# A mixture-of-experts trunk layer on one core: routing's order, low parts on GpSimd, and two weight slots opened earlier

## The chip, the core and the metric

The program runs on one core of one Trainium2 chip. The metric is the device time of one execution in microseconds, given as the median of several runs. The engines are called TensorE (PE in the rows), VectorE (DVE), ScalarE (ACT), GpSimd (POOL) and SyncE (SP, which here issues the weights' DMAs); PEld is TensorE's weight load, and a q behind a name (SPq, ACTq) is the queue of that engine, DMA issues above all.

## The reference

One layer works on 512 latent tokens of 1024 features, with 256 context tokens beside them. What lies ahead of the change is the normed input projection, three token mixers and their gated merge. The part around the change is the output projection with its residual, the second norm, the routing and the experts:

```python
mix_l = merge_branches((pool, att_l, rwo_l), gate_l, w_br[l], w_out[l])   # ... merged @ w_out
x = x + mod[:, 2] * mix_l
f_l = modulate(x, norm2_g[l], mod[:, 3], mod[:, 4]).reshape(B * L, D)     # rms_norm(x, g) * (1 + scale) + shift
x = x + mod[:, 5] * hier_moe(f_l, w_rg, w_re, w_g, w_u, w_d)

def hier_moe(h, ...):
    lg = h @ w_rg                                  # 4 groups: the best one
    grp = argmax(lg); p_grp = softmax(lg)[grp]
    le = (h @ w_re).reshape(T, 4, 8)[grp]          # 8 experts in it: the best two
    top_v, top_i = top_k(le, 2)
    gates = p_grp * softmax(top_v)
    # each chosen expert: (silu(x @ w_g[e]) * (x @ w_u[e])) @ w_d[e], times its gate, summed by token
```

There are 32 experts; each has w_g and w_u of 1024 x 512 and w_d of 512 x 1024, float32, so 6 MB a piece and 201 MB in all.

## The kernel before, in words

**The sum.** The merged branches stand transposed in SBUF, split in a high part `mgh` (in two of the weight slots, the names ew_8461 and ew_8462 in rows) and a low part `mgl` (tiles mq), each 8 blocks of 128 features by 512 tokens. The output projection is `out_mm` (L1446 before): for four column blocks of 256, `wo[0]` to `wo[3]`, and four groups of 128 tokens (t = 0 to 3) it adds three products per block k, high x high, low x high and high x low. `out_add` (L1452 to L1454) multiplies by the gate row, adds to the residual `xt2[t]` and lets ScalarE sum the squares of these 256 columns (`sq`). Blocks 2 and 3 of the weights lie in the tiles xn0 and xn1.

**Routing.** `turned` transposes the four (later the next four) 128 x 128 blocks of token group t on TensorE (L1369), and ScalarE copies them (L1370) to `fT[t]`, a tile of the ring F (5 buffers, pool `wfa`). `logits` (L1376) multiplies them by the router's weights. `route` takes rsqrt on GpSimd (L104), scales the logits (L1385) and chooses the group and two experts in a row of small VectorE operations up to L1401. `count` (L1409, L1410) gives each token its place in its expert's 64 rows. `normed` (L1436, L1437, L1440, L1441) writes the normed tokens as a high and a low part to xn0 (t = 0, 1) or xn1 (t = 2, 3), and a plain copy in an F tile to `x_d` in DRAM, from which later experts' tokens are gathered. xn1 is free only when the last column block's matmuls are done. For the first four experts, tokens are not gathered but chosen by matmuls with a one-hot matrix (`chosen` L1500, `rows_of` L1506), scaled by `put` and given to the experts.

**The experts' weights.** `load` issues one half of one matrix of one expert (128 x 2048 floats) on SP's queue (L1257). Thirteen places take turns by the list RING: slots ew0 to ew7 in one pool, ew8 and ew9 where `mgh` lies, ew10 and ew11 in a pool `peq` that is opened where `mgl` and the ring F lay, and place 12 in two tiles of another ring. Two further halves (SPARE) go into tiles that the experts need only later (oh, yhl, xT). `fetch(n)` issues up to the n-th half; after the first round each place is filled again when its expert's matmuls are done. `up` (L1608) is an expert's first product, `down` (L1643) its last.

**What sets the order.** The program is written in order and a scheduler places each instruction in its engine's queue; `tc.high_priority(n)` lets what is written inside it stand ahead of other work, the more the greater n. Each engine works its queue in order. SP's queue is in the order in which the loads are written.

Of the kernel before, what the change touches and what calls it, by code (L numbers as in the profile page):

```python
# [9 lines left out]
FT = mybir.dt.float32  # L10
# [68 lines left out]
def trunk_kernel(ctx: ExitStack, tc: tile.TileContext, I, out, dbg=None, upto=99):  # L79
# [665 lines left out]

    pb = ctx.enter_context(ExitStack())
    TW = dict(bufs=1, reuse_waits="tile")
    pf_ = ctx.enter_context(ExitStack())

    wfb = ctx.enter_context(tc.tile_pool(name="rmapg", side="right", **TW))  # L750
    wfa = pf_.enter_context(tc.tile_pool(name="rmapf", side="right", **TW))

    class Ring:
        n = 0
# [468 lines left out]
    m5 = xpool2.tile([128, D], FT)  # L1223
    m2 = mgp.tile([128, D], FT, name="m2", bufs=1)

    RING = (4, 5, 6, 7, 12, 0, 1, 2, 3, 8, 9, 10, 11)
    NS = len(RING)

    SPARE = (4, 5)
# [199 lines left out]
    def normed(t):  # L1429

        if t % 2 == 0:
            xns.append(xnp.tile([128, 2, 2, D], FR, name=f"xn{t // 2}"))
        hi, lo = xns[t // 2][:, 0, t % 2], xns[t // 2][:, 1, t % 2]
        for h in range(2):
            sl = slice(h * 512, h * 512 + 512)
            S.activation(hi[:, sl], xt2[t][:, sl], AF.Copy, scale=ss[:, t, 3:4])  # L1436
        V.scalar_tensor_tensor(lo, xt2[t], ss[:, t, 3:4], hi.bitcast(FT), op0=OP.mult, op1=OP.subtract)  # L1437

        xf = wfa.tile([128, D], FT, name="F", bufs=7 - FB)
        S.activation(xf, xt2[t], AF.Copy, scale=ss[:, t, 3:4])  # L1440
# [53 lines left out]
    def gather(b):  # L1494

        oh = (ep if b else xnp).tile([128, 4, EB, 64], FR, name="oh", bufs=1)
        ohf = oh.rearrange("p t e s -> p t (e s)")

        def chosen(t):
            return V.tensor_tensor(oh[:, t], slot[:, t, b * EB:b * EB + EB, None].to_broadcast([128, EB, 64]),  # L1500
                                   io1[:, None, :].to_broadcast([128, EB, 64]), OP.is_equal)

        def rows_of(p, k, ts):
            for t in ts:
                for a in range(2):
                    PE.matmul(p, xns[t // 2][:, a, t % 2, k * 128:k * 128 + 128], ohf[:, t], start=(t == 0 and a == 0),  # L1506
                              stop=(t == 3 and a == 1))

        def put(k, p):
            if k % 2:  # L1510
                S.activation(xT[:, k], p, AF.Identity, scale=g2c[:, k:k + 1], bias=s2c[:, k:k + 1])
            else:
                V.tensor_scalar(xT[:, k], p, g2c[:, k:k + 1], s2c[:, k:k + 1], op0=OP.mult, op1=OP.add)

        if b == 0:

            ahead = {}
            for t in range(3):
                chosen(t)
                yield  # L1520
            for k in range(AH):
                ahead[k] = ps_big()[:, 0:EB * 64]
                rows_of(ahead[k], k, range(3))
            chosen(3)
            yield
            xT = ep.tile([128, KD, EB * 64], FT, name="xT")
            for k in range(KD):
                p = ahead[k] if k in ahead else ps_big()[:, 0:EB * 64]
                rows_of(p, k, (3,) if k in ahead else range(4))
                put(k, p)  # L1530
            yield xT, *slots(b, oh)
            return
        for t in range(4):
            chosen(t)
        yield
        gc, ix = slots(b, oh)
        ii = ep.tile([128, EB // 2], U32, name="ii")
# [7 lines left out]
        xT = ep.tile([128, KD, EB * 64], FT, name="xT")  # L1545
# [12 lines left out]
    nxt = gather(0)  # L1558
    for t in range(4):
        p = ps_big()[:, 0:256]  # L1560
        for k in range(KD):
            out_mm(p, wo[2], t, k)
        turned(t, 0, 4)
        out_add(p, t, 2)
    for t in range(5):
        if t < 4:
            p = ps_big()[:, 0:256]
            for k in range(KD):
                out_mm(p, wo[3], t, k)
            out_add(p, t, 3)  # L1570
        if t:
            with tc.high_priority(0):
                turned(t - 1, 4, 4)
                logits(t - 1, 0, 8)
                if t > 1:
                    count(t - 2)
                route(t - 1)
            normed(t - 1)
        if t > 1:
            next(nxt)  # L1580
# [5 lines left out]
    if upto < 7:  # L1586
        return
    dump("slot", slot)
    fetch(11)
    gates()  # L1590
    m2x.close()
    mgx.close()
    pf_.close()
    peq = ctx.enter_context(tc.tile_pool(name="expq", side="right", **TW))
    fetch(NS)
    epx = ctx.enter_context(ExitStack())
    ep = epx.enter_context(tc.tile_pool(name="experts", bufs=2, reuse_waits="tile"))
    tgx = ep.tile([128, 4, NE // 2, 6], FR, bufs=1)

    tp = tg.rearrange("p t (q e) -> p t q e", e=2)  # L1600
# [4 lines left out]
    def up(xT, w, pg, i):  # L1605
        for k in range(KD):
            for h in range(2):
                PE.matmul(pg[64 * h:64 * h + 64, i], xT[:, k], of(w[i], k)[:, h * 256:h * 256 + 256],  # L1608
                          start=(k == 0), stop=(k == KD - 1), tile_position=(0, 64 * h))

    def hidden(pg, pool):
# [43 lines left out]
    def parts_of(y, h, rows, pool, name="yhl", eng=G):  # L1655

        sl = slice(h * 512, h * 512 + 512)
        yhl = pool.tile([rows, 2, 512], FR, name=name, bufs=1)
        yh, yl = yhl[:, 0], yhl[:, 1]
        S.activation(yh, y[:, sl], AF.Copy)  # L1660
        eng.tensor_sub(yl, y[:, sl], yh.bitcast(FT))  # L1661
        return sl, yh, yl

    def combine(y, ix, last=False):

        oT = oT_
        V.tensor_scalar(oT, iol, ix, None, op0=OP.is_equal)
        if last:
            yield
            with tc.high_priority(100):  # L1670
                pts = [parts_of(y, h, 128, ep, *(("oh", G) if h else ("yhl", V))) for h in range(2)]
# [6 lines left out]
        pt_ = parts_of(y, 0, 128, ep)  # L1678
        yield
        for t in range(4):  # L1680
            add(oT, t, *pt_)
        pt_ = parts_of(y, 1, 128, ep)
        yield
        for t in range(4):
            add(oT, t, *pt_)
# [1 line left out]
    def store(t):  # L1687
        nc.sync.dma_start(out[t * 128:(t + 1) * 128], xt2[t])

    load(SPARE[0], *(ep.tile([128, 1, D], FT, name=nm, bufs=1) for nm in ("oh", "yhl")))  # L1690
    load(SPARE[1], ep.tile([128, 2, D], FT, name="xT"))
# [15 lines left out]
    for e in range(NE + 1):  # L1707
        fetch(NS + max(0, 6 * e - 2) - (2 if e > 1 else 0))
        j = e % EB
        if e < NE:  # L1710
            if j == 0:
                got[e // EB] = cur
                nxt = gather(e // EB + 1) if e + EB < NE else iter(())
            xT = got[e // EB][0][:, :, j * 64:j * 64 + 64]
# [37 lines left out]
    with tc.If(nmost > 64):  # L1752
        for t in range(4):
            if t % 2 == 0:
                xns.append(xnp.tile([128, 2, 2, D], FR, name=f"xn{t // 2}"))
            xf = op_.tile([128, D], FT, name="xf")
            nc.sync.dma_start(xf, x_d[t * 128:(t + 1) * 128])
            S.activation(xns[-1][:, 0, t % 2], xf, AF.Copy)
            V.tensor_sub(xns[-1][:, 1, t % 2], xf, xns[-1][:, 0, t % 2].bitcast(FT))
        with tc.For_i(0, NE, 1) as e:  # L1760
# [12 lines left out]
            with tc.For_i(0, 7, 1):  # L1773
# [18 lines left out]
                y = op_.tile([64, D], FT)  # L1792
                pg = ps_big().rearrange("p (i n) -> p i n", i=2)
                up(xT, wo, pg, 0)
                up(xT, wo, pg, 1)
                down(turn_(hidden(pg, op_), op_), wo, gc, y, 0)
                oT = op_.tile([64, 512], FR)
                pt = ps_sm()[0:64]
# [1 line left out]
                    PE.transpose(pt[:, t * 128:t * 128 + 128], oh[:, t].bitcast(FT), ident)  # L1800
                S.activation(oT, pt, AF.Copy)
                for h in range(2):
                    pt_ = parts_of(y, h, 64, op_)
                    for t in range(4):
                        add(oT, t, *pt_)
        for t in range(4):
# [114 lines left out]
```

## Time and profile before

| what | value |
|---|---|
| runs | 1447.19, 1440.27 and 1447.98 us; median 1447.19 us |
| the profiled execution | 1448.53 us, span 1446.6 us |
| busy share: TensorE, its weight load, VectorE, ScalarE, GpSimd | 94%, 70%, 57%, 33%, 26% |
| moved by DMA | 399.96 MB, 276 GB/s over the span |
| mean granted TensorE clock | 0.977 of full speed |

The span is the time from the first to the last instruction on the core; the rest of an execution lies around it. A busy share is a mean over stages that have different limits: up to some 970 us the mixers and the sum run, behind that the experts.

### The profile page before, as it was taken

Reading aid. Unit: us, or ns where it says so; the run is one execution under the profiler, and the core shown is the slowest. Engines: PE = TensorE matmul, PEld = TensorE weight load, DVE = VectorE, ACT = ScalarE, POOL = GpSimd, SP = SyncE. Lnnn points to the kernel's source line nnn. Section 1 sums busy time; section 2 is a strip of 40 time slices with the busy share of each in tenths; the row PEclk is TensorE's granted clock in tenths of the full one; section 3 lists DMA queues with packets and bytes.
Section 4 is the critical chain, followed back from the end, with each engine's and each line's share of the span. In section 5 each row is a group of like instructions: output and inputs, shape, how many; then the busy total and the mean of one; then the engine's idle time right before and its main releaser. Section 6 shows DMA issues by size and latency. Waiting matters only on the chain.

```text
span 1446.6 us, 24032 instructions
## 1 busy us (share of the span) xinstructions
PE 1362.2 (94%) x9148; PEld 1018.7 (70%) x9148; DVE 822.0 (57%) x1673; ACT 482.5 (33%) x1089; POOL 382.5 (26%) x345
## 2 busy tenths in 40 slices
PE   5999999998999999799999998999999999999897
PEld 3786788887888888688887776985555554555443
DVE  4553327779988958266776886462433433333334
ACT  4432235665565632144445523341111111111101
POOL 2111155445432444112221257110101101111001
PEclk9999999999999999799999999999999999999999
DMA  9368755666566466965847276579999999999996
GB/s 367 151 216 309 236 181 171 215 210 199 193 217 217 179 206 214 252 209 159 260 136 240 85 259 234 204 277 417 419 418 418 419 419 419 419 418 419 419 419 241
DMA packets 138038, 399.96 MB, mean 276 GB/s; under 512 B 38757, under 2 KB 69477, under 8 KB 107200
## 3 DMA queue, kind: packets, MB, share of 16 engines
q1 hardware_dynamic: 101920, 331.55, 61.9%
q10 hardware_dynamic: 32400, 58.60, 11.1%
q0 software_dynamic: 3600, 8.24, 1.7%
q8 instruction: 74, 1.21, 0.3%
q14 instruction: 44, 0.36, 0.1%
HBM read 343.44 MB, written 58.72 MB: 278 GB/s over the span
## 4 chain that ended last, share of the span: by engine, by line
PE 42%; DMA 25%; DVE 8%; issue 3%; ACT 2%; POOL 1%; SPq 1%; ACTq 0%; DVEq 0%; POOLq 0%
DMA ew<-in_w_eu_dram 9%; DMA ew<-in_w_ed_dram 5%; PE pp L220 5%; PE pp L1608 5%; DMA ew<-in_w_eg_dram 4%; PE pp L1152 3%; PE pp L1446 3%; PE pp L1643 2%; PE pp L234 2%; PE sc L1007 2%; PE pp L825 1%; PE pp L812 1%; PE sc L1006 1%; DMA F<-in_w_eg_dram 1%; PE pp L818 1%
## 5 line engine op out<-in xcount | busy, mean ns | idle before, releaser
L1608 PE MATMUL pp<-ew,xT 128*64 128x256 f32 x1888 | 225.0, 383 | 14.4 <-DMA ew<-in_w_eu_dram 9.4
L1608 PEld LDWEIGHTS pp<-ew,xT 128*64 128x64 f32 x1888 | 132.0, 137 | 97.4 <-issue 18.5
L220 PE MATMUL pp<-xlh,wh 128*128 128x512 f32 x344 | 135.7, 405 | 1.3 <-ACT wide L413 1.3
L220 PE MATMUL pp<-xll,wh 128*128 128x512 f32 x344 | 135.7, 395 | 0.4 <-POOL xll L320 0.4
L220 PE MATMUL pp<-xlh,wl 128*128 128x512 f32 x344 | 135.1, 393 | 0.0
L1661 POOL TENSOR_TENSOR yhl<-m,yhl 128x512 fp32r<-128x512 f32 x30 | 38.2, 1272 | 364.0 <-ACT yhl L1660 364.0
L215 POOL TENSOR_TENSOR wl<-wraw,wh 128x512 fp32r<-128x512 f32 x84 | 113.4, 1377 | 64.1 <-ACT wh L214 59.9
L1653 DVE TENSOR_TENSOR x<-x,pp 128x512 f32<-128x512 f32 x128 | 80.7, 681 | 41.6 <-PE pp L1652 41.5
L1643 PE MATMUL pp<-ew,hT 128*64 128x512 f32 x440 | 101.0, 599 | 0.0
L1614 DVE TENSOR_TENSOR hh<-hh,pp 128x256 f32<-128x256 f32 x32 | 13.5, 421 | 148.1 <-ACT hh L1613 148.1
L1646 DVE SCALAR_TENSOR_TENSOR m<-pp,gc,m 64x512 f32<-64x512 f32 x62 | 46.5, 750 | 63.3 <-PE pp L1643 62.6
L220 PEld LDWEIGHTS pp<-xlh,wh 128*128 128x128 f32 x344 | 64.7, 190 | 20.8 <-issue 5.6
L214 ACT ACTIVATE wh<-wraw 128x512 fp32r<-128x512 f32 (+1 forms) x112 | 61.1, 612 | 54.1 <-PE pp L220 51.7
L220 PEld LDWEIGHTS pp<-xll,wh 128*128 128x128 f32 x344 | 65.2, 190 | 15.1 <-issue 2.0
L220 PEld LDWEIGHTS pp<-xlh,wl 128*128 128x128 f32 x344 | 65.2, 189 | 13.8
L1643 PEld LDWEIGHTS pp<-ew,hT 128*64 128x64 f32 x440 | 29.0, 136 | 55.9 <-issue 50.9
L234 PE MATMUL pp<-wh,xlh 128*128 128x256 f32 x192 | 59.5, 310 | 5.1 <-ACT qo L659 2.3
L806 POOL TENSOR_TENSOR ao<-ar,cst 128x512 f32<-128x512 f32 x24 | 30.8, 1284 | 124.3 <-PE pp L818 68.3
L1622 ACT ACTIVATE hT<-psm 128x256 f32<-128x256 f32 x32 | 12.3, 384 | 149.7 <-PE psm L1620 144.2
L1613 ACT ACTIVATE hh<-pp 128x256 f32<-128x256 f32 x32 | 12.3, 384 | 139.9 <-PE pp L1608 139.9
L234 PE MATMUL pp<-wl,xlh 128*128 128x256 f32 x192 | 57.7, 300 | 0.0
L234 PE MATMUL pp<-wh,xll 128*128 128x256 f32 x192 | 57.5, 299 | 0.0
(436 smaller groups left out, 3133.4 us busy)
## 6 DMA issues: line engine op xcount, KB each, us to landing
ew<-in_w_eg_dram SPq DMA_DIRECT2D x59, 1024.0 KB
ew<-in_w_eu_dram SPq DMA_DIRECT2D x58, 1024.0 KB
ew<-in_w_ed_dram SPq DMA_DIRECT2D x56, 1024.0 KB
wraw<-in_w_in_dram SPq DMA_DIRECT2D x27, 1024.0 KB
u_d<-ub ACTq DMA_DIRECT2D x16, 1152.0 KB
wada<-in_w_adr_dram SPq DMA_DIRECT2D x16, 1024.0 KB
ar<-u_d SPq DMA_DIRECT2D x24, 640.0 KB
wa<-in_w_ad_dram SPq DMA_DIRECT2D x8, 1024.0 KB
```

The costliest lines, as they stand in the source:

```text
L214: S.activation(self.h[:, kk, :n], raw[:, kk, :n], AF.Copy)
L215: (eng[q % 2] if type(eng) is tuple else eng).tensor_sub(self.l[:, kk, :n], raw[:, kk, :n], self.h[:, kk, :n].bitcast(FT))
L220: PE.matmul(ps, a[:, k, cs], b[part][:, k], start=(k + n == 0), stop=(k == KD - 1 and n == 2))
L234: PE.matmul(ps, a[part][:, k, ts], b[:, k], start=(n == 0), stop=(n == 3 * KD - 1))
L806: G.tensor_mul(ao, aa[:, :, 2:3].to_broadcast([128, 4, 2, 64]), offm[:, None].to_broadcast([128, 4, 2, 64]))
L1152: PE.matmul(ps, a[:, k], bs[k][:, x], start=(c == 0), stop=(c == 11))
L1446: PE.matmul(p, a[:, ts], x[:, k], start=(k == 0 and c == 0), stop=(k == KD - 1 and c == 2))
L1608: PE.matmul(pg[64 * h:64 * h + 64, i], xT[:, k], of(w[i], k)[:, h * 256:h * 256 + 256], start=(k == 0), stop=(k == KD - 1), tile_position= ...
L1643: PE.matmul(pd[64 * h:64 * h + 64], hT[:, k], of(w[2], k)[:, h * 512:h * 512 + 512], start=(k == 0), stop=(k == 3), tile_position=(0, 64 * h))
L1646: V.scalar_tensor_tensor(y[ps_, h * 512:h * 512 + 512], pd[64 * h:64 * h + 64], gc, m5[ps_, h * 512:h * 512 + 512], op0=OP.mult, op1=OP.mult)
L1653: V.tensor_add(xt2[t][:, sl], xt2[t][:, sl], p)
L1661: eng.tensor_sub(yl, y[:, sl], yh.bitcast(FT))
```

## The change

Four groups of edits.

1. The low parts' products with the last column block's weights (`mgl` x `wo[3][0]`, 32 matmuls) are done first, ahead of block 2, into four accumulators that stay open; the high parts follow block 2. With that `mgl` is read out after block 2, its pool is closed there and `peq` opened, and `fetch(11)` stands there and no longer behind the routing. Slots 10 and 11 come ahead of 8 and 9 in RING.
2. The priority of the routing's second half (`turned`, `logits`, `count`, `route`) rises from 0 to 100, and that of `chosen(3)` and the first experts' rows to 200.
3. The low parts of tokens 2 and 3 (`normed`) are made by GpSimd in two halves, out of the F tile and the high part, and no longer by VectorE.
4. The ring F stays open to the end; the experts' transposed tokens (`xT`, now two tiles for each of two turns), the low and high parts of an expert's result (`yhl`) and one of the spare halves lie in it.

```diff
-    RING = (4, 5, 6, 7, 12, 0, 1, 2, 3, 8, 9, 10, 11)
+    RING = (4, 5, 6, 7, 12, 0, 1, 2, 3, 10, 11, 8, 9)
...
-        V.scalar_tensor_tensor(lo, xt2[t], ss[:, t, 3:4], hi.bitcast(FT), op0=OP.mult, op1=OP.subtract)
+        if t < 2:
+            V.scalar_tensor_tensor(lo, xt2[t], ss[:, t, 3:4], hi.bitcast(FT), op0=OP.mult, op1=OP.subtract)
...
         S.activation(xf, xt2[t], AF.Copy, scale=ss[:, t, 3:4])
+        if t > 1:
+            for h in range(2):
+                sl = slice(h * 512, h * 512 + 512)
+                G.tensor_sub(lo[:, sl], xf[:, sl], hi[:, sl].bitcast(FT))
         nc.scalar.dma_start(x_d[t * 128:(t + 1) * 128], xf)
...
-            chosen(3)
+            with tc.high_priority(200):
+                chosen(3)
             yield
-            xT = ep.tile([128, KD, EB * 64], FT, name="xT")
-            for k in range(KD):
-                p = ahead[k] if k in ahead else ps_big()[:, 0:EB * 64]
-                rows_of(p, k, (3,) if k in ahead else range(4))
-                put(k, p)
+            xT = xTs[b % 2]
+            with tc.high_priority(200):
+                for k in range(KD):
+                    p = ahead[k] if k in ahead else ps_big()[:, 0:EB * 64]
+                    rows_of(p, k, (3,) if k in ahead else range(4))
+                    put(k, p)
...
     nxt = gather(0)
+
+    pss = [ps_big()[:, 0:256] for _ in range(4)]
     for t in range(4):
-        p = ps_big()[:, 0:256]
+        for k in range(KD):
+            PE.matmul(pss[t], mgl[k][:, t * 128:t * 128 + 128], wo[3][0][:, k], start=(k == 0), stop=False)
+    for t in range(4):
+        p = (ps_sm() if t else ps_big())[:, 0:256]
         for k in range(KD):
             out_mm(p, wo[2], t, k)
         turned(t, 0, 4)
         out_add(p, t, 2)
+    mgx.close()
+    peq = ctx.enter_context(tc.tile_pool(name="expq", side="right", **TW))
+    fetch(11)
     for t in range(5):
         if t < 4:
-            p = ps_big()[:, 0:256]
             for k in range(KD):
-                out_mm(p, wo[3], t, k)
-            out_add(p, t, 3)
+                for c in range(2):
+                    PE.matmul(pss[t], mgh[k][:, t * 128:t * 128 + 128], wo[3][c][:, k], start=False,
+                              stop=(k == KD - 1 and c == 1))
+            out_add(pss[t], t, 3)
         if t:
-            with tc.high_priority(0):
+            with tc.high_priority(100):
                 turned(t - 1, 4, 4)
                 logits(t - 1, 0, 8)
...
-    fetch(11)
     gates()
     m2x.close()
-    mgx.close()
-    pf_.close()
-    peq = ctx.enter_context(tc.tile_pool(name="expq", side="right", **TW))
     fetch(NS)
...
+    spare = wfa.tile([128, 1, D], FT, name="F", bufs=7 - FB)
+    xTs = [[wfa.tile([128, KD // 2, EB * 64], FT, name="F", bufs=7 - FB) for _ in range(2)] for _ in range(2)]
+    yhl_ = []
```

On ScalarE's queue, this is the stretch from token 1's norm to the store of token 3, before. F<-psm is a copy of transposed rows, xn_9623 the tile of tokens 2 and 3's high parts, F<-x a plain normed copy, x_d<-F its store, sq a sum of squares:

```order
L1440 ACTIVATE F<-x_8917,ss 128x1024
L1454 ACTIVATE sq,ss<-x_8918 128x256
L1441 DMA x_d<-F 128x1024
L1440 ACTIVATE F<-x_8918,ss 128x1024
L1441 DMA x_d<-F 128x1024
L1436 ACTIVATE xn_9623<-x_8918,ss 128x512 x2
L1696 DMA m_9817<-in_iota_dram 128x512
L1454 ACTIVATE sq,ss<-x_8918 128x256
L1370 ACTIVATE F<-psm 128x512 x2
L1436 ACTIVATE xn_9623<-x_8918,ss 128x512 x2
L1440 ACTIVATE F<-x_8918,ss 128x1024
L1441 DMA x_d<-F 128x1024
```

and after:

```order
L1458 ACTIVATE sq,ss<-x_8918 128x256
L1440 ACTIVATE F<-x_8917,ss 128x1024
L1445 DMA x_d<-F 128x1024
L1717 DMA m_9821<-in_iota_dram 128x512
L1458 ACTIVATE sq,ss<-x_8918 128x256
L1435 ACTIVATE xn_9631<-x_8918,ss 128x512 x2
L1440 ACTIVATE F<-x_8918,ss 128x1024
L1435 ACTIVATE xn_9631<-x_8918,ss 128x512 x2
L1440 ACTIVATE F<-x_8918,ss 128x1024
L1445 DMA x_d<-F 128x1024
L1369 ACTIVATE F<-psm 128x512 x2
L1445 DMA x_d<-F 128x1024
```

The copies of the transposed rows of tokens 2 and 3 (L1370 before, L1369 after) stood ahead of token 3's norm; they now stand behind both norms and a store.

On SP's queue, these are the weights from the place where two loads wait for the sum, up to the first load into a slot used a second time (the last row), before; ew is a slot, mosti the counts that SP reads:

```order
L1257 DMA ew_9714<-in_w_eg_dram 128x2048
L1257 DMA ew_9716<-in_w_eu_dram 128x2048
L1257 DMA ew_9738<-in_w_eu_dram 128x2048
L1257 DMA ew_9740<-in_w_ed_dram 128x2048
L1257 DMA oh<-in_w_ed_dram 128x1024
L1257 DMA yhl<-in_w_ed_dram 128x1024
L1257 DMA xT<-in_w_ed_dram 128x2048
L1751 TENSOR_LOAD mosti
L1751 ISA x2
L1257 DMA ew_9867<-in_w_ed_dram 128x2048
```

and after:

```order
L1256 DMA ew_9429<-in_w_eg_dram 128x2048
L1256 DMA ew_9431<-in_w_eu_dram 128x2048
L1256 DMA ew_9739<-in_w_eu_dram 128x2048
L1256 DMA ew_9741<-in_w_ed_dram 128x2048
L1256 DMA F<-in_w_ed_dram 128x1024 x3
L1256 DMA oh<-in_w_ed_dram 128x1024
L1772 TENSOR_LOAD mosti
L1772 ISA x2
L1256 DMA ew_9871<-in_w_ed_dram 128x2048
```

The first two rows were slots 8 and 9, free when the whole sum is done, and are now slots 10 and 11, free when the low parts are read; slots 8 and 9 follow. The spares stand behind all of these in both, and the load into a slot used again behind the counts.

On GpSimd's queue, the stretch from the norms' rsqrt to the first gather, before:

```order
L104 TENSOR_TENSOR ss<-ss,nhalf 128x1 x4
L1701 MEMSET xn_9820 128x2048
L1701 MEMSET xn_9821 128x2048
L1541 DMA xn_9821<-x_d,ii 128x1024 x2
L1661 TENSOR_TENSOR yhl<-m_9916,yhl 128x512 x2
```

and after:

```order
L104 TENSOR_TENSOR ss<-ss,nhalf 128x1 x4
L1444 TENSOR_TENSOR xn_9631<-F,xn_9631 128x512 x4
L1722 MEMSET xn_9824 128x2048
L1722 MEMSET xn_9825 128x2048
L1548 DMA xn_9825<-x_d,ii 128x1024 x2
```

Four subtractions of 128 x 512 (L1444) stand behind the four rsqrt; on VectorE's queue two operations of 128 x 1024 (L1437) are gone.

## Rows read from the trace of the kernel before

**Rows 1.** The windows, whole core: busy us, instructions, TensorE clock, DMA share, GB/s

```profile
925.00:950.00 25.00, 25.00 (x217) 25.00 (x215) 11.89 (x40) 12.26 (x27) 1.64 (x3) 1.00 0.26 104
950.00:975.00 25.00, 24.20 (x204) 21.44 (x204) 17.12 (x77) 9.60 (x17) 4.11 (x3) 1.00 0.86 331
975.00:1000.00 25.00, 24.93 (x185) 14.61 (x181) 6.32 (x18) 1.92 (x5) 2.16 (x2) 1.00 1.01 417
...
1300.00:1400.00 100.00, 92.89 (x612) 49.78 (x614) 36.05 (x62) 12.82 (x27) 10.89 (x9) 1.00 1.01 419
```

**Rows 2.** The timeline of SP, the weights' queue, 922 to 971 us

```profile
922.23 26.73 SPq L1257 DMA_DIRECT2D ew<-in_w_eg_dram  x2
950.96 10.73 SPq L1257 DMA_DIRECT2D ew<-in_w_eu_dram  x2
...
963.43 0.43 SPq L1257 DMA_DIRECT2D xT<-in_w_ed_dram  x1
970.90 0.34 SPq L1257 DMA_DIRECT2D ew<-in_w_ed_dram  x1
```

**Rows 3.** The chain of waits, 935 to 972 us: start, length, what

```profile
935.07 5.70 PE pp L1446 x48
...
953.36 0.61 ACT F L1370
954.01 1.10 PE pp L1376 x8
955.13 0.27 DVE lgs L1385
...
955.99 1.28 DVE xn L1437
...
960.79 1.08 PE psm L1409 x8
...
968.99 3.17 PE pp L1608 x27
```

**Rows 4.** The timeline of ScalarE, 938 to 976 us

```profile
940.29 1.34 ACT L1436 ACTIVATE xn<-x,ss 128x512 fp32r<-128x512 f32 x2 [0.85 <-POOL ss L104]
941.54 1.14 ACT L1440 ACTIVATE F<-x,ss 128x1024 f32<-128x1024 f32 x1
...
942.70 0.33 ACTq L1441 DMA_DIRECT2D x_d<-F  x1
943.05 0.41 ACT L1454 ACTIVATE sq<-x 128x256 f32<-128x256 f32 x1
943.36 0.19 ACT L1454 ACTIVATION_READ_ACCUMULATOR sq<-x 128x1 f32 x1
...
950.96 0.72 ACT L1436 ACTIVATE xn<-x,ss 128x512 fp32r<-128x512 f32 x1 [1.30 <-PE pp L1446]
```

**Rows 5.** The timeline of VectorE, 936 to 970 us

```profile
937.95 0.42 DVE L1452 TENSOR_TENSOR tm<-pp,m 128x256 f32<-128x256 f32 x1 [1.42 <-PE pp L1446]
...
957.19 0.25 DVE L1385 SCALAR_TENSOR_TENSOR lgs<-pp,ss,lb 128x36 f32<-128x36 f32 x1
```

**Rows 6.** The timeline of VectorE, one operation at two places

```profile
223.69 0.14 DVE L666 TENSOR_SCALAR st<-st 128x4 f32<-128x4 f32 x1
...
331.43 1.23 DVE L666 TENSOR_SCALAR st<-st 128x4 f32<-128x4 f32 x1
```

**Rows 7.** The timeline of GpSimd at the second of these places

```profile
329.87 2.77 POOL L215 TENSOR_TENSOR wl<-wraw,wh 128x512 fp32r<-128x512 f32 x2
```

**Rows 8.** The page's costliest groups, GpSimd's subtraction of the experts

```profile
L1661 POOL TENSOR_TENSOR yhl<-m,yhl 128x512 fp32r<-128x512 f32 x30 | 38.2, 1272 | 364.0 <-ACT yhl L1660 364.0
```

**Rows 9.** The windows around an idle TensorE, columns as in rows 1

```profile
880.40:883.60 3.20, 0.00 (x0) 0.00 (x0) 3.13 (x5) 1.15 (x2) 3.20 (x3) 0.86 0.57 182
883.60:886.10 2.50, 2.06 (x4) 1.25 (x5) 0.47 (x1) 0.63 (x1) 2.50 (x2) 0.50 0.37 108
...
889.50:893.00 3.50, 3.50 (x16) 2.89 (x16) 3.01 (x4) 1.50 (x3) 1.45 (x2) 1.00 0.29 75
```

More of the change, by code (lines that the diff above doesn't have):

```diff
@@ L747, in trunk_kernel @@
     TW = dict(bufs=1, reuse_waits="tile")
-    pf_ = ctx.enter_context(ExitStack())
     wfb = ctx.enter_context(tc.tile_pool(name="rmapg", side="right", **TW))
-    wfa = pf_.enter_context(tc.tile_pool(name="rmapf", side="right", **TW))
+    wfa = ctx.enter_context(tc.tile_pool(name="rmapf", side="right", **TW))
     class Ring:
@@ L1509, in put @@
         def put(k, p):
+            x = xT[k // 4][:, k % 4]
             if k % 2:
-                S.activation(xT[:, k], p, AF.Identity, scale=g2c[:, k:k + 1], bias=s2c[:, k:k + 1])
+                S.activation(x, p, AF.Identity, scale=g2c[:, k:k + 1], bias=s2c[:, k:k + 1])
             else:
-                V.tensor_scalar(xT[:, k], p, g2c[:, k:k + 1], s2c[:, k:k + 1], op0=OP.mult, op1=OP.add)
+                V.tensor_scalar(x, p, g2c[:, k:k + 1], s2c[:, k:k + 1], op0=OP.mult, op1=OP.add)
         if b == 0:
@@ L1544, in gather @@
         yield
-        xT = ep.tile([128, KD, EB * 64], FT, name="xT")
+        xT = xTs[b % 2]
         for k in range(0, KD, 2):
@@ L1607, in up @@
             for h in range(2):
-                PE.matmul(pg[64 * h:64 * h + 64, i], xT[:, k], of(w[i], k)[:, h * 256:h * 256 + 256],
+                PE.matmul(pg[64 * h:64 * h + 64, i], xT[k], of(w[i], k)[:, h * 256:h * 256 + 256],
                           start=(k == 0), stop=(k == KD - 1), tile_position=(0, 64 * h))
@@ L1653, in add, with parts_of @@
         V.tensor_add(xt2[t][:, sl], xt2[t][:, sl], p)
-    def parts_of(y, h, rows, pool, name="yhl", eng=G):
+    def parts_of(y, h, yhl, eng=G):
+        if yhl is yhl_:
+            if not yhl_:
+                yhl_.append(wfa.tile([128, 2, 512], FR, name="F", bufs=7 - FB))
+            yhl = yhl_[0]
         sl = slice(h * 512, h * 512 + 512)
-        yhl = pool.tile([rows, 2, 512], FR, name=name, bufs=1)
         yh, yl = yhl[:, 0], yhl[:, 1]
@@ L1670, in combine @@
             with tc.high_priority(100):
-                pts = [parts_of(y, h, 128, ep, *(("oh", G) if h else ("yhl", V))) for h in range(2)]
+                pts = [parts_of(y, h, ep.tile([128, 2, 512], FR, name="oh", bufs=1) if h else yhl_, G if h else V)
+                       for h in range(2)]
             for h in range(2):
@@ L1677, in combine @@
             return
-        pt_ = parts_of(y, 0, 128, ep)
+        pt_ = parts_of(y, 0, yhl_)
         yield
@@ L1681, in combine @@
             add(oT, t, *pt_)
-        pt_ = parts_of(y, 1, 128, ep)
+        pt_ = parts_of(y, 1, yhl_)
         yield
@@ L1688, in store @@
         nc.sync.dma_start(out[t * 128:(t + 1) * 128], xt2[t])
-    load(SPARE[0], *(ep.tile([128, 1, D], FT, name=nm, bufs=1) for nm in ("oh", "yhl")))
-    load(SPARE[1], ep.tile([128, 2, D], FT, name="xT"))
+    load(SPARE[0], ep.tile([128, 1, D], FT, name="oh", bufs=1), spare)
+    load(SPARE[1], *(x.rearrange("p (o k) n -> p o (k n)", o=1) for x in xTs[1]))
     cur = next(nxt)
@@ L1713, in trunk_kernel @@
                 nxt = gather(e // EB + 1) if e + EB < NE else iter(())
-            xT = got[e // EB][0][:, :, j * 64:j * 64 + 64]
+            xT = [got[e // EB][0][k // 4][:, k % 4, j * 64:j * 64 + 64] for k in range(KD)]
             pg = ps_big().rearrange("p (i n) -> p i n", i=2)
@@ L1755, in trunk_kernel @@
                 xns.append(xnp.tile([128, 2, 2, D], FR, name=f"xn{t // 2}"))
-            xf = op_.tile([128, D], FT, name="xf")
+            xf = wfa.tile([128, D], FT, name="F", bufs=7 - FB)
             nc.sync.dma_start(xf, x_d[t * 128:(t + 1) * 128])
@@ L1791, in trunk_kernel @@
                 V.tensor_copy(gc, pi)
-                y = op_.tile([64, D], FT)
+                y = wfa.tile([128, D], FT, name="F", bufs=7 - FB)[0:64]
                 pg = ps_big().rearrange("p (i n) -> p i n", i=2)
-                up(xT, wo, pg, 0)
-                up(xT, wo, pg, 1)
+                up([xT[:, k] for k in range(KD)], wo, pg, 0)
+                up([xT[:, k] for k in range(KD)], wo, pg, 1)
                 down(turn_(hidden(pg, op_), op_), wo, gc, y, 0)
@@ L1802, in trunk_kernel @@
                 for h in range(2):
-                    pt_ = parts_of(y, h, 64, op_)
+                    pt_ = parts_of(y, h, wfa.tile([128, 2, 512], FR, name="F", bufs=7 - FB)[0:64])
                     for t in range(4):
```

## The prediction

> **What bounds the kernel now.** I read the stretches of the span first, then the DMA queue of the weights, then the chain of waits back from the experts. The experts are bound by their weights: from 975 us on the DMA share is 1.01 at 417 to 419 GB/s, while TensorE is busy for 92.89 of 100 us in a late stretch [rows 1]. The reader is to see that a full DMA queue, not an engine, carries the time from there to the end. The stream has a fixed length: 32 experts of 6 halves are 192 halves of 128 x 2048 floats (1.049 MB), which at 419 GB/s take 2.50 us each. Fifteen halves have a place before any place must be used twice (13 slots and 2 spares); the other 177, 443 us of transfers and over, can only follow once places come free.
>
> So what counts is when that stream starts. SP issues the weights in order [rows 2]. Its two issues that end at 961.69 us had waited for TensorE and for a store; the last spare is issued at 963.43 us; the next weight, into a place used a second time, goes out at 970.90 us. It waits for expert 0's first matmuls, which begin at 968.99 us [rows 3]. Before that the DMA engines are mostly idle: a share of 0.26 from 925 to 950 us [rows 1]. Whatever moves expert 0's start moves the stream and, with it, the end. Whatever only fills the idle stretch before it moves nothing.
>
> What sets expert 0's start is the chain [rows 3]: the last column block of the sum on TensorE; ScalarE's copies of the transposed rows (953.36 us); the logits of tokens 2 and 3 (954.01 us); the routing's small VectorE operations from 955.13 us, with one low part of 1.28 us among them (955.99 us); the count (960.79 us); the rows of expert 0. From the copies to expert 0 it is 15.63 us.
>
> **The change part by part.** (a) *Slots.* Two of the weights that SP held in its rows of 26.73 and 10.73 us [rows 2] can load while block 3 is still summed, since the low parts are read out early. That is two halves, 5.0 us of transfers, put into a stretch in which the DMA engines are idle. But both have a place before and after; the number of halves that follow the first second use stays 177, and that use still waits for expert 0's matmuls. I cost the gain at 0. Were it all on the path it would be worth 5.0 us (below).
>
> (b) *The sum's order.* The same matmuls stand in another order. One takes 5.70/48 = 0.119 us [rows 3]. Token 0's last block had 24 of its own behind block 2; now 32 low parts stand ahead of block 2 and 16 behind it, so it ends 24 x 0.119 = 2.9 us later, near 941 us in place of 937.6 with the logits' first matmuls that now stand between. The sum's end moves little: it is the same work, with part of the logits behind it now, so about 949.7 us.
>
> (c) *ScalarE's order* decides most. Before, the copies of tokens 2 and 3 stand ahead of token 3's norm and run at 953.36 us. After, both norms and a store stand ahead of them in the same queue. From the multiplication at 937.95 us to the first norm at 940.29 us is 2.3 us [rows 4, 5], so the queue of norms starts near 941 + 0.3 + 2.3 = 943.7 us. Ahead of the copies it now holds four norms (1.34 + 1.14 each, 9.9 us), three squares with their read (0.6 each, 1.8), two copies of the first tokens (0.61 each, 1.2 [rows 3]) and four DMA issues (0.33 each, 1.3): 14.2 us, and some 14.1 as neighbours overlap by up to 0.1 us here and there [rows 4]. The copies start near 957.8 us, 4.5 us later than at 953.36. The lowest it can be: tokens 2 and 3's norms write where the last column block's weights lie, so they wait for the sum's end, as the row at 950.96 us does now [rows 4]; 949.7 plus two norms and an issue, 5.3 us, is 955.0, 1.6 us later. The highest, without overlap and with token 0's norm half a microsecond behind my reckoning, is 5.0. The queue is filled without a hole from token 0 on, so I take 4.5. The logits behind the copies cost what they cost now.
>
> (d) *Low parts on GpSimd.* VectorE loses its 1.28 us operation inside the chain. By itself that is a gain of 1.28 us; but token 3's routing, which filled the time around it, now runs beside token 2's from the start: between 957.19 us (token 3's first operation) [rows 5] and 960.79 nothing gets shorter, and only the 2.06 us between the two tokens' first operations shrinks, to some 1.5. I take -0.5 (from -1.3 to 0). Against that GpSimd now does four subtractions of 128 x 512, each 1.27 us by the nearest row, the experts' own [rows 8], about 5.1 us in all, from the third norm's end (some 955.5 us) into the routing after 960 us. What they cost VectorE the rows show: the same 128x4 operation takes 0.14 us alone and 1.23 us at 331.43, where it ends with GpSimd's subtraction [rows 6, 7]. One such wait is 1.1 us, two 2.2, none 0 if the routing comes behind all four. I take 1.0.
>
> [...]
>
> (e) *TensorE's clock.* With the copies late, TensorE has nothing for some 2 to 3 us after the sum's end, which it does not have now. [...] Behind the new gap lie the logits of tokens 2 and 3 (1.10 us [rows 3]) and later counts of 1.08. At half the clock each costs about its own length again: 0 to 2.2 us, and I take 1.0.
>
> (f) *Experts' tiles in the F ring*, and the transposed rows in two tiles: no instruction is added. The ring's former readers are the stores and the copies above, done before expert 0's rows. 0; the cover is that the first writes into those tiles come behind the count, and if it fails the price is the wait for the last of those stores, today a part of SP's row of 10.73 us [rows 2].
>
> Expert 0 starts 4.5 - 0.5 + 1.0 + 1.0 = 6.0 us later, near 975.0 us. Today's first second use goes out 1.9 us behind expert 0's start and lands behind the last spare's transfer, so it has some tenths of slack; I take 0.5 off. The stream and the end move by 5.5 us: 1448.53 + 5.5 = 1454.0 for the profiled execution, which stands 1.34 us above the median of the three runs; against that, 1447.19 + 5.5 = 1452.7.
>
> **The rivals.** *The prefetch decides.* If the stream's length rather than its start counts, two halves fewer lie in it: -5.0 us, with the 1.28 us of the low part off the chain -6.3: 1441 to 1442. The idle DMA share of 0.26 speaks for it [rows 1]; that SP's next issue waits for expert 0's matmuls and not for the spares speaks against it. It decides if expert 0 starts no later than now and the first second use no longer waits for it. Chance 0.10, with 0.04 faster by over 0.5%.
>
> *The queue on ScalarE is shorter than I read it.* If the copies wait only for the sum's end (1.6 us late) and the routing meets no subtraction, it is 1.6 - 0.5 = +1.1, about 1448.3. For it speaks that ScalarE waits 1.30 us for the sum's end now [rows 4]; against it that two tokens' norms now come together. Chance 0.15.
>
> *The slow case.* The clock stays at half through the rows of expert 0, 44 matmuls of some 0.12 us (+5.4), with two blocked operations: about +11, 1458. TensorE's busy stretch behind the gap speaks against it. Chance 0.08.
>
> [...]
>
> **How the numbers follow.** A difference under 0.5%, 7.2 us, can't be told from none here: the three runs lie 7.7 us apart. My forecast has 0.67 and spans +3 to +9 us (each term at its nearer bounds), 1450 to 1456; about a third of it lies above +7.2. Faster: 0.04. Slower: 0.22 of the forecast and 0.08 of the slow case, 0.30. Same: 0.66. The range from 1444 to 1459 leaves out the prefetch case and the worst of the slow one.
>
> **What would show it.** Right: ScalarE's copies of tokens 2 and 3 at 957 to 959 us, behind both norms; a gap on TensorE before the logits; a VectorE operation of routing at over 1 us while GpSimd subtracts; expert 0's first matmul at 973 to 977; two weights issued before 945; and from there the DMA share at 1.0 to the end, all of it later by the same amount. Wrong: expert 0 at 969 or before, a clock of 0.50 after 970, or a hole in the stream among the experts, which would make (f) a cost.

## The result and the profile after

The changed kernel took 1455.05 us (median of 8 runs, 1447.62 to 1459.24) against 1444.71 us (median of 8, 1440.27 to 1447.98). The ratio is 1.0065, with a 95% interval of 1.0043 to 1.0087: some 9.4 us slower, between 6.2 and 12.6 (the medians themselves lie 10.3 us apart). That lies in the forecast range and on its side. By the prediction's own mark of 0.5%, though, I had given 0.66 to no difference that can be told and 0.30 to a slower kernel; the measured 0.65% lies above that mark, and its interval, 0.43 to 0.87%, on both sides of it. The forecast 1452.7 was too low, and, as the rows show, much of the reason was another than the one I put first.

The profiled execution took 1455.28 us, with a span of 1453.2. Two executions are compared best from a common point, since the instructions are the same up to the end of column block 1 and the two still arrive there 5.95 us apart. That point is the first matmul that reads the tiles xn, in the timelines of TensorE before and after:

```profile
921.77 0.28 PE L1446 MATMUL pp<-xn,ew 128*128 128x256 f32 x1
```

```profile
915.82 2.40 PE L1570 MATMUL pp<-xn,mq 128*128 128x256 f32 x19
```

From there to expert 0's first matmul I call the stage, and from there to the end of the span the measure. Before, the stage is 968.99 - 921.77 = 47.2 us and the measure 1446.6 - 921.77 = 524.8 us. After, expert 0 starts at 975.76 in the chain of waits (start, length, what):

```profile
944.83 0.34 DVE tm L1456
...
948.86 1.15 DVE rt L1400
950.01 0.11 DVE slot L1409
950.15 1.34 DVE oh L1504
951.49 0.04 issue
951.53 1.65 PE pp L1510 x6
953.18 3.26 PE pp L1375 x16
956.44 3.14 PE pp L1510 x14
959.58 1.13 PE psm L1408 x6
...
960.99 1.92 PE psm L1408 x8
...
970.53 5.22 PE pp L1510 x24
975.76 2.87 PE pp L1624 x25
```

So the stage is 975.76 - 915.82 = 59.9 us (+12.7) and the measure 1453.2 - 915.82 = 537.4 (+12.6). From expert 0 to the end it is 477.4 us against 477.6: everything is lost ahead of expert 0, and the stream of weights carries it to the end unchanged. The reader is to see in the chain that from 951.53 us on it is TensorE almost without a hole. The eight matmuls of the last count take 1.92 us where they took 1.08 [rows 3]. TensorE's timeline has the wait ahead of this, and the windows tell why (columns as in rows 1):

```profile
948.33 0.61 PE L1408 MATMUL psm<-rt,cst 128*128 128x32 f32 x2 [1.80 <-DVE rt L1400]
```

```profile
943.80:946.50 2.70, 2.70 (x26) 2.62 (x24) 2.70 (x15) 1.80 (x5) 0.81 (x1) 1.00 0.86 267
946.50:948.30 1.80, 0.03 (x1) 0.00 (x0) 1.70 (x15) 1.80 (x3) 0.55 (x1) 0.97 1.07 396
948.30:951.50 3.20, 3.06 (x14) 2.95 (x14) 3.06 (x7) 3.20 (x6) 2.82 (x3) 0.50 0.94 342
...
970.00:973.00 3.00, 3.00 (x15) 3.00 (x16) 0.67 (x4) 0.45 (x1) 0.00 (x0) 0.50 0.03 5
973.00:975.70 2.70, 2.70 (x16) 2.57 (x15) 0.55 (x1) 0.11 (x1) 0.63 (x1) 0.54 0.00 0
975.70:978.00 2.30, 2.30 (x23) 1.58 (x24) 1.09 (x1) 2.19 (x3) 2.30 (x2) 1.00 0.01 4
```

At the sum's end TensorE waits 1.80 us for VectorE's routing of tokens 0 and 1; its granted clock is 0.50 behind that wait, and stays so almost to expert 0 (the window up to 975.70 us has 0.54), although the engine is shown busy nearly all the time. The weights had been waiting too: over 950 to 975 us the DMA share is 0.47, where it was 0.86 [rows 1], and from 970 to 973 us it is 0.03.

### The profile page after: what moved, and what is told of

The parts are those of the page before. It is cut to its first block, busy times and chain, and to the rows that moved or that the text cites. A ratio compares the mean times of both kernels' runs of the same rounds, so it can differ in the third digit from the quotient of the medians.

```text
span 1453.2 us, 24044 instructions
## 1 busy us (share of the span) xinstructions
PE 1369.8 (94%) x9148; PEld 1027.7 (71%) x9148; DVE 819.0 (56%) x1671; ACT 483.0 (33%) x1089; POOL 388.0 (27%) x349
## 4 chain that ended last, share of the span: by engine, by line
PE 49%; DMA 18%; DVE 8%; issue 3%; ACT 2%; POOL 1%; SPq 1%; ACTq 0%; DVEq 0%; POOLq 0%
PE pp L1624 9%; DMA ew<-in_w_eu_dram 5%; PE pp L220 5%; DMA ew<-in_w_ed_dram 4%; PE pp L1659 4%; PE pp L1151 3%; DMA ew<-in_w_eg_dram 3%; PE pp L1450 2%; PE pp L234 2%; PE sc L1006 2%; PE pp L1667 2%; PE pp L824 1%; PE sc L1005 1%; PE pp L811 1%; DMA F<-in_w_eg_dram 1%
## 5 line engine op out<-in xcount | busy, mean ns | idle before, releaser
L1624 PE MATMUL pp<-ew,F 128*64 128x256 f32 x1888 | 225.9, 385 | 12.6 <-DMA ew<-in_w_eu_dram 7.8
L1624 PEld LDWEIGHTS pp<-ew,F 128*64 128x64 f32 x1888 | 133.1, 137 | 95.6 <-issue 19.1
L1681 POOL TENSOR_TENSOR F<-m,F 128x512 fp32r<-128x512 f32 x30 | 38.2, 1273 | 363.1 <-ACT F L1680 359.2
```

The source lines that it names most:

```text
L1624: PE.matmul(pg[64 * h:64 * h + 64, i], xT[k], of(w[i], k)[:, h * 256:h * 256 + 256], start=(k == 0), stop=(k == KD - 1), tile_position=(0, ...
```

## The experiments

Each is the profile of one execution unless a ratio is given, so a difference of some tenths of a microsecond decides nothing. The measure is taken as above, the clock from the windows.

| kernel | stage | measure | against before |
|---|---|---|---|
| before | 47.2 | 524.8 | |
| changed | 59.9 | 537.4 | +12.6 |
| changed, 32 useless transposes | 56.9 | 534.4 | +9.6 |
| changed, 60 useless transposes | 52.0 | 530.1 | +5.3 |
| the same, low parts on VectorE | 52.0 | 529.5 | +4.7 |
| changed, low parts on VectorE | 60.3 | 538.1 | +13.3 |
| changed, old priorities | 60.2 | 540.0 | +15.2 |
| changed, old order of the sum | 57.3 | 535.4 | +10.6 |
| before, ring F alone | 47.1 | 525.3 | +0.5 |
| before, ring and GpSimd's low parts | 49.5 | 530.0 | +5.2 |
| before, ring and priorities | 53.2 | 531.6 | +6.8 |
| before, ring and new sum | 57.0 | 537.0 | +12.2 |
| before, token 2 earlier | 53.2 | 531.4 | +6.6 |
| before, one wait added | 62.9 | 541.7 | +16.9 |

In three of these (the ring alone, the ring with GpSimd, the ring with the new sum) some rows of expert 0's group stand behind its first matmul, so there the measure counts and not the stage.

My theory after the result: the half clock carries the loss, and TensorE's waits for routing bring it. The rivals: VectorE's waits on GpSimd (the expectations name a port as what makes them; no run shows that it is one), the queue on ScalarE, the priorities, or the sum's order by themselves.

**Useless transposes in the gap.** Their results are read by nobody.

```diff
                 logits(t - 1, 0, 8)
+                if t == 2:
+                    pf = ps_sm()
+                    for _ in range(32):
+                        PE.transpose(pf[:, 0:128], fT[1][:, 7], ident)
                 if t > 1:
                     count(t - 2)
```

> The changed kernel with 32 transposes of no use (128x128, 0.11 us each at full clock, into a PSUM tile of their own) on TensorE between the end of the sum and the first count, where it stood idle for 1.80 us and where its clock fell to 0.50. Measure: the stage from the first matmul behind column block 1 to expert 0's first matmul, 47.2 us before and 59.9 after. If the half clock carries the loss, TensorE stays at 1.00 there and the stage is 50 to 54 us. If VectorE's waits on GpSimd or the queue on ScalarE carry it, the stage stays at 58 or more, whatever the clock.

The stage was 56.9, between the two. The clock held where the transposes stood and fell further on. TensorE's timeline there, with the waits in brackets, and two windows:

```profile
959.41 0.85 PE L1408 MATMUL psm<-rt,cst 128*128 128x32 f32 x6 [0.52 <-DVE rt L1400]
961.09 2.50 PE L1510 MATMUL pp<-oh,xn 128*128 128x256 f32 x10 [0.82 <-DVE oh L1504]
```

```profile
957.50:960.00 2.50, 1.98 (x17) 1.70 (x15) 2.27 (x21) 0.22 (x1) 0.00 (x0) 1.00 0.87 231
960.00:965.00 5.00, 4.18 (x22) 4.07 (x21) 2.74 (x15) 0.21 (x1) 0.00 (x0) 0.57 0.76 265
```

In windows of one microsecond the first under 1.00 is that from 960 to 961, at 0.83: the clock fell in the second of two waits, neither as long as the 1.80 us of the first. Neither theory was settled, so the later waits had to be covered too.

**More of them.** 28 further transposes, written ahead of the last count.

```diff
     with tc.high_priority(100):
+        pf4 = ps_sm()
+        for _ in range(28):
+            PE.transpose(pf4[:, 0:128], fT[3][:, 6], ident)
         count(3)
```

> The first filler kernel held TensorE at 1.00 up to about 960.8 us, where two waits for VectorE (0.52 and 0.82 us) stood, and was then at 0.50 to about 974. Here 28 more transposes of no use stand behind the logits of tokens 2 and 3, where those waits were. If the half clock carries what is left, the clock stays at 1.00 to expert 0 and the stage (47.2 us before, 59.9 after, 56.9 with the first fillers) is 49 to 52 us. If the order and the waits for VectorE carry it, the stage stays at 55 or more with the clock at 1.00.

The clock was 1.00 in every window to expert 0, and the stage 52.0 us, at the edge of what the clock theory gave:

```profile
960.00:965.00 5.00, 4.92 (x44) 4.72 (x42) 3.37 (x17) 0.21 (x1) 0.00 (x0) 1.00 0.80 260
965.00:970.00 5.00, 5.00 (x45) 5.00 (x44) 2.66 (x9) 1.58 (x3) 0.15 (x1) 1.00 0.10 38
```

60 transposes of no use make the kernel 7.3 us faster by the measure. The stretch from the last count to expert 0 shows what the clock is worth by itself, since there the instructions and their order are those of the changed kernel. TensorE's timeline with the clock held:

```profile
962.07 1.08 PE L1408 MATMUL psm<-rt,cst 128*128 128x32 f32 x8
...
970.20 1.08 PE L1631 MATMUL pp<-ew,F 128*64 128x256 f32 x8
```

That is 8.1 us, where the changed kernel takes 975.76 - 960.99 = 14.8 and the kernel before 8.2: 6.6 us of the 12.6 are the half clock's in this stretch alone. Ahead of the last count the transposes cost time of their own, and with them the scheduler set eight of the rows later; so how the remaining 5.3 us are shared between the new order and the transposes is not shown.

**One wait, and no work.** The reverse test on the kernel before: the count of token 0 reads its choice from a copy made by DMA.

```diff
         pc = pl["c"][:, NE * t:NE * t + NE]
+        r0 = rt[:, 0]
+        if t == 0:
+            r0 = rp.tile([128, NE], FT, name="r0", bufs=1)
+            nc.gpsimd.dma_start(r0, rt[:, 0])
         for q in reversed(range(t + 1)):
-            PE.matmul(pc, K("upper") if q == t else K("ones"), rt[:, q], start=(q == t), stop=(q == 0))
+            PE.matmul(pc, K("upper") if q == t else K("ones"), rt[:, q] if t else r0, start=(q == t), stop=(q == 0))
```

> The kernel before with one wait added on TensorE and no work: token 0's count reads its choice from a copy that a small DMA on GpSimd's queue makes (128 x 32 floats), so TensorE has to wait for it behind the sum. If a wait costs only itself, the measure is 524.8 plus the wait, 525 to 528 us. If a wait of 1 us or more there lets the clock fall and the rows behind it run at half clock, it is 5 us or more longer than the wait alone, 531 to 538.

The copy took longer than I had meant:

```profile
952.37 0.61 PE L1413 MATMUL psm<-r,cst 128*128 128x32 f32 x2 [5.12 <-DMA r<-rt]
...
974.09 5.25 PE L1510 MATMUL pp<-oh,xn 128*128 128x256 f32 x24
```

```profile
956.00:970.00 14.00, 13.72 (x66) 13.58 (x65) 7.03 (x44) 0.43 (x2) 0.00 (x0) 0.50 0.77 265
970.00:979.00 9.00, 9.00 (x44) 9.00 (x44) 2.96 (x9) 1.69 (x3) 0.17 (x1) 0.50 0.14 57
```

The measure is 16.9 us longer, 11.8 more than the wait. With no other edit than the wait the rows of expert 0's group run at 0.50 to their end. (The scheduler also moved six rows of token 0 ahead of the last logits, as in the changed kernel, so whatever this move costs is in the 11.8 us too.)

**The parts of the change taken back.** Low parts on VectorE:

```diff
-        if t < 2:
-            V.scalar_tensor_tensor(lo, xt2[t], ss[:, t, 3:4], hi.bitcast(FT), op0=OP.mult, op1=OP.subtract)
+        V.scalar_tensor_tensor(lo, xt2[t], ss[:, t, 3:4], hi.bitcast(FT), op0=OP.mult, op1=OP.subtract)
...
-        if t > 1:
-            for h in range(2):
-                sl = slice(h * 512, h * 512 + 512)
-                G.tensor_sub(lo[:, sl], xf[:, sl], hi[:, sl].bitcast(FT))
```

> The changed kernel with the low parts of tokens 2 and 3 back on VectorE and none on GpSimd. VectorE's operations of 1.15, 1.34 and 1.24 us in the routing of tokens 0 and 1 should be at 0.2 and 0.4 again. If the port is the cause, the stage is 53 to 56 us. If the clock is, TensorE is idle in the same place ahead of the first subtraction, the clock falls all the same, and with two operations of 1.28 us on VectorE the stage is 57 to 61 us.

60.3, as the clock theory had it: the three operations are at 0.19 and 0.42 us again, TensorE waits 2.96 us for VectorE at the sum's end, the clock is 0.92 in the window with the gap (950.0 to 952.5 us) and 0.50 behind it. No subtraction is needed for that.

Old priorities (100 and 200 to 0):

> The changed kernel with the priorities of before (0 for routing's second half, none above for the chosen rows). If the priorities put routing late, the stage is 48 to 52 us. If the order of the sum does, token 1's logits still stand behind the sum and the rows of token 0 ahead of the logits of tokens 2 and 3, TensorE is idle at the sum's end, the clock falls and the stage is 56 to 61 us.

60.2, with 0.50 from 952.5 us on, as the theory of the sum's order had it: the new priorities aren't needed for the loss. The old order of the sum (the loops of before in place of the new ones, the two slots opened behind the routing):

> The changed kernel with the sum in the order of before (the low parts inside each column block, the two slots opened behind the routing); priorities, GpSimd's low parts and the ring F as changed. If the sum's order causes the loss, token 0's and 1's logits stand inside the sum again, TensorE has no gap over 1.5 us at its end, the clock stays at 1.00 and the stage is 47 to 51 us. If GpSimd's subtractions or the priorities cause it, the stage is 55 us or more.

57.3, against my expectation of 47 to 51: this theory, that the loss needs the new order of the sum, fell. The logits of tokens 0 and 1 did stand inside the sum again, and TensorE was at 1.00 up to 955 us; from there the clock is 0.76, 0.50 and 0.50 in windows of one microsecond, with waits of 0.57 and 0.19 us ahead of it. Then, with GpSimd subtracting, a chosen row on VectorE came late:

```profile
959.43 2.50 PE L1510 MATMUL pp<-oh,xn 128*128 128x256 f32 x10 [2.29 <-DVE oh L1504]
```

The ten rows behind that wait take 2.50 us at half clock, so here a wait and the clock both cost.

**The parts one at a time, on the kernel before.** The same diffs the other way round. The ring F alone:

> The kernel before with edit 4 alone (the experts' tiles in the ring F; RING's new order, slots opened behind the routing as before). The order on TensorE, ScalarE and VectorE up to expert 0's rows is that of before. If the ring costs nothing, the stage is 47 to 48.5 us and the stretch from expert 0 to the end 477 to 478.5. If the ring makes the experts wait, that stretch is over 480.

Measure 525.3 (+0.5), 478.3 us from expert 0 to the end: the ring costs nothing. With GpSimd's low parts:

> The kernel before with edit 4 and GpSimd's low parts of tokens 2 and 3, with the old sum and the old priorities. On TensorE the rows of token 0 now stand ahead of the last logits of tokens 2 and 3, the rest is the order of before. If GpSimd's port alone is enough to let TensorE wait and its clock fall, the stage is 53 to 58 us with 0.50 in it. If it needs the new sum's order, the clock stays at 1.00 and the stage is 46 to 49.

530.0 (+5.2); the stage of 49.5 us lies in neither of the two ranges, though the clock does fall. TensorE waits 0.97 us for a VectorE operation of routing at 945.60 us; the clock is 1.00 to 948, then at 0.50 to 951 and once more from 955 to 958. With the priorities:

> The kernel before with edit 4 and the new priorities (100 and 200), with the old sum and the low parts on VectorE. If the priorities alone put the routing where TensorE waits for it, the stage is 53 to 58 us with a clock of 0.50 in it; if they need the new sum or GpSimd's subtractions, the stage is 46 to 49 us at 1.00.

531.6 (+6.8). The clock is 0.89 from 952 to 953 us, where TensorE had waited 0.33 us, and 0.50 behind that, with a wait of 1.22 us on the way. With the new sum:

> The kernel before with edit 4 and the new order of the sum, its early slots included; old priorities, low parts on VectorE. Measured from the first matmul that reads the tiles xn to the end of the span: 524.8 us before, 537.4 after. The new order alone puts the last logits of tokens 0 and 1 behind the sum. If that is enough to make TensorE wait and its clock fall, this is 532 to 538 us. If it takes GpSimd or the priorities too, 525 to 528.

537.0 (+12.2), behind two waits of over 2 us, between which the clock had come back (0.50 from 952 to 954 us, 1.00 from 955 to 961):

```profile
951.30 0.61 PE L1408 MATMUL psm<-rt,cst 128*128 128x32 f32 x2 [2.10 <-DVE rt L1400]
...
961.88 1.92 PE L1408 MATMUL psm<-rt,cst 128*128 128x32 f32 x8 [2.11 <-DVE slot L1409]
```

The three costs are 4.7, 6.3 and 11.7 above the ring alone and sum to 22.7, where all together cost 12.1 above it. They don't add up. In each of them the clock falls on the way to expert 0, and a stretch can be at half only once; I take that for the reason.

**GpSimd at an even clock.** The 60 transposes, low parts on VectorE.

> The kernel with the useless transposes that held the clock at 1.00 (530.1 us by the same measure), with the low parts of tokens 2 and 3 back on VectorE. At an even clock this shows what GpSimd's subtractions are worth by themselves. If the port's waits cost more than VectorE's two operations of 1.28 us, it is 527.5 to 529.5; if VectorE's own operations cost more, 530.5 to 532.

529.5 against 530.1, the upper end of the range for waits on GpSimd that cost more. At 1.00 throughout, GpSimd's subtractions and VectorE's two operations come out the same within 0.6 us, which one execution of each can't tell from nothing.

**Token 2 earlier.** An attempt at a version that beats both: in the kernel before, token 2's last transposes are written into token 3's block, and the rest of that block is held behind them.

```diff
-            for k in range(KD):
+            for k in range(4 if t == 3 else KD):
                 out_mm(p, wo[3], t, k)
+            if t == 3:
+                with tc.high_priority(0):
+                    tr = turned(2, 4, 4)
+                with tc.issue_after(tr.ins):
+                    for k in range(4, KD):
+                        out_mm(p, wo[3], t, k)
             out_add(p, t, 3)
...
-                turned(t - 1, 4, 4)
+                if t != 3:
+                    turned(t - 1, 4, 4)
```

> The kernel before with the second-half transposes of token 2 held ahead of the last 12 matmuls of token 3 on TensorE, so that token 2 is routed while token 3 is still summed. If expert 0's start sets the end, the measure is 522 to 524 us (524.8 before) and the time 0.1 to 0.2% less, under what a comparison can tell. If the wait for token 0's count ahead of token 3's last matmuls is longer than what it saves, or the clock falls, it is 525 to 533.

It is slower: measure 531.4, ratio 1.0031 (1.0013 to 1.0049). The clock was 0.65 and 0.66 from 952.5 to 957.5 us, back at 1.00, and 0.51 and 0.50 from 960 to 970, though no wait behind the sum was over 0.6 us. No version here beats the kernel before.

## Why the prediction was right in sign and range, and where it was wrong

*What bounds the kernel* and *slots*: right. Expert 0 starts later and the end follows to 0.2 us. SP issued two more weights early, by its timeline (start, length, what) at 933.23 and 933.60 us, then waited for the sum with the next, and the first weight into a used place went out 1.92 us behind expert 0's start, as before:

```profile
933.23 0.33 SPq L1256 DMA_DIRECT2D ew<-in_w_eg_dram  x1
933.60 9.73 SPq L1256 DMA_DIRECT2D ew<-in_w_eu_dram  x2
...
977.68 0.34 SPq L1256 DMA_DIRECT2D ew<-in_w_ed_dram  x1
```

The earlier loads only moved the idle stretch of the DMA engines: the DMA share over 925 to 950 us is 0.51 in place of 0.26, and over 950 to 975 us 0.47 in place of 0.86. The slack of 0.5 us that I took off wasn't there: start and end moved alike.

*ScalarE's order* (term 4.5): the queue is as I read it, both norms and a store ahead of the copies:

```profile
938.27 1.34 ACT L1435 ACTIVATE xn<-x,ss 128x512 fp32r<-128x512 f32 x2 [0.85 <-POOL ss L104]
...
950.71 0.57 ACT L1369 ACTIVATE F<-psm 128x512 f32<-128x512 f32 x1
...
951.18 0.58 ACT L1369 ACTIVATE F<-psm 128x512 f32<-128x512 f32 x1
```

From the common point the first copy comes at 34.9 us in place of 31.6, 3.3 later, inside my bounds of 1.6 to 5.0. But it isn't in the chain. The logits, ready to go at 951.8, start at 953.18, since six rows of token 0 stand ahead of them on TensorE and wait for VectorE. The wait for VectorE, in the routing of tokens 0 and 1, I hadn't put on the path at all.

*Low parts on GpSimd* (term 1.0): VectorE's waits on GpSimd are there, and earlier than I put them, in the routing of tokens 0 and 1. GpSimd and VectorE, from their timelines:

```profile
948.68 5.34 POOL L1444 TENSOR_TENSOR xn<-F,xn 128x512 fp32r<-128x512 f32 x4 [1.52 <-ACT F L1440]
```

```profile
947.99 0.19 DVE L1400 TENSOR_TENSOR rt<-oo 128x32 f32<-128x32 f32 x1
...
948.86 1.15 DVE L1400 TENSOR_TENSOR rt<-oo 128x32 f32<-128x32 f32 x1
949.93 0.18 DVE L1409 SCALAR_TENSOR_TENSOR slot<-psm,rt 128x32 f32<-128x32 f32 x1
950.15 1.33 DVE L1504 TENSOR_TENSOR oh<-slot,cst 128x256 fp32r<-128x256 f32 x1
951.43 0.19 DVE L1409 SCALAR_TENSOR_TENSOR slot<-psm,rt 128x32 f32<-128x32 f32 x1
951.65 1.24 DVE L1504 TENSOR_TENSOR oh<-slot,cst 128x256 fp32r<-128x256 f32 x1
```

The same operation takes 0.19 us and 0.87 us later 1.15. Three operations lose 1.15 + 1.33 + 1.24 less 0.19 and twice 0.42, 2.7 us, above my upper bound of 2.2 and below the 5.1 that I had reckoned for the four subtractions together. One subtraction at a time is waited for: by GpSimd's timeline in shorter windows the first three end at 949.96, 951.19 and 952.61 us, and the three operations 0.05, 0.29 and 0.28 us behind them. Not every operation is held: the two of L1409, at 949.93 and 951.43 us, take 0.18 and 0.19 us while the subtractions run; why, no run shows. Yet with the low parts on VectorE the measure was 0.7 us longer in the changed kernel and 0.6 shorter with the clock held, no gain that can be told.

*TensorE's clock* (term 1.0, from 0 to 2.2): this is the step that failed. I costed the half clock for two groups of some 1.1 us, because in the rows that I went by, where TensorE was idle from 880.40 to 883.60 us, the clock was 0.50 behind the gap and back at 1.00 from 889.50 on, 6 us after it [rows 9]. The 1.0 itself no run shows; in its place the runs show the 6.6 us that follow. Here the clock wasn't back for over 25 us. The stretch from the last count to expert 0, the same instructions in both, went from 968.99 - 960.79 = 8.2 us [rows 3] to 14.8 us; that alone is 6.6 us, and with the clock held it is 8.1 again. Of my own signs of being wrong one came true, the clock of 0.50 after 970. That the clock stays at half up to expert 0 stood in the prediction as the slow case, with +11 us and a chance of 0.08, and against it I named TensorE's busy stretch behind the gap. That reason was wrong.

*The sum's order* (b): I took it for 2.9 us on token 0 and no cost in itself. With the ring alone beside it it costs 12.2 us, the most of the three. It puts the last logits of tokens 0 and 1 behind the sum; that this is the reason is argued, and the old sum with the other edits cost 10.6 all the same.

*The ring F*: 0 forecast, +0.5 measured in one execution.

So the sum of +5.5 came as near to the measured +9.4 as it did partly by luck: its largest term isn't in the chain, one was put in the wrong place, and one was six times too small. Luck too is that expert 0's first matmul stands at 975.76 us, inside my 973 to 977: this execution reached the common point 5.95 us earlier, and from there expert 0 starts 12.7 us later, where I had added up 6.0.

That the profiled execution shows +12.6 from the common point and the timed runs between 6.2 and 12.6 stays open, since only one execution of the changed kernel was traced. The mean clock over the span, which is on record for each of its eight runs, points at a fall that isn't the same in all: it is 0.978 and 0.975 in the two fastest, of 1447.62 and 1450.08 us, and 0.967 and 0.968 in the two slowest, of 1458.28 and 1459.24. It was 0.977 in the profiled execution before and 0.968 in the one after.

## What to carry to other kernels

Where TensorE works through small instructions between waits, ask of each reordering not only what it delays but what it does to TensorE's clock: with one wait added and no work, the wait cost 5.1 us and what followed, at half clock, 11.8. Before you credit an earlier load, look for what the first load that can't be early waits for; if that wait stays, the load only fills an idle stretch. And try the parts of a change one at a time before adding up their costs: here parts of 4.7, 6.3 and 11.7 us make 12.1 together.

## What I had not expected of the hardware

A TensorE that is shown as busy can stay at half clock. From 970 to 973 us after the change it is busy for 3.00 of 3.00 us at 0.50, and with the added wait for 9.00 of 9.00. What it ran there were rows of 256 columns, with a few matmuls of 6 and 32 columns among them; after the change 1.00 came back at the end of the last 24 rows.

Nor does the fall need a long wait. The kernel with the ring alone has the order of before and on TensorE no wait over 0.28 us behind the sum, only logits of 36 columns, transposes, counts and rows; it lost the clock all the same and had it back 3 us later, with a measure only 0.5 us longer:

```profile
949.00:950.00 1.00, 1.00 (x11) 1.00 (x11) 0.91 (x5) 1.00 (x2) 0.00 (x0) 1.00 0.96 389
950.00:951.00 1.00, 1.00 (x10) 0.97 (x8) 1.00 (x3) 0.49 (x1) 0.00 (x0) 0.84 1.00 414
951.00:952.00 1.00, 1.00 (x5) 0.68 (x4) 1.00 (x10) 0.00 (x0) 0.00 (x0) 0.50 1.07 408
...
954.00:955.00 1.00, 0.87 (x8) 0.76 (x7) 0.24 (x3) 0.00 (x0) 0.00 (x0) 0.95 0.96 401
```

And a wait as long as that after the sum can leave it alone. In the kernel before, among the experts, TensorE waited 1.81 us for weights and kept 1.00, by its timeline and the windows:

```profile
1344.36 1.95 PE L1608 MATMUL pp<-ew,xT 128*64 128x256 f32 x16 [1.81 <-DMA ew<-in_w_eu_dram]
```

```profile
1342.50:1344.40 1.90, 0.09 (x4) 0.04 (x2) 0.00 (x0) 0.00 (x0) 0.00 (x0) 1.00 1.02 414
1344.40:1348.00 3.60, 3.60 (x24) 2.44 (x24) 1.23 (x3) 0.39 (x1) 0.00 (x0) 1.00 1.02 419
```

So in the order of before, too, the clock can fall behind the sum, and here the length of a wait alone doesn't say whether it does. That the half clock costs what it costs is shown, by holding it and by one wait; which of the waits and narrow instructions make it fall, and why it came back after 3 us in some kernels and after 25 in others, stays open.
